# A two-layer hybrid decoder step on one core: all weight chunks rounded on ScalarE, all remainders made on VectorE

## The chip, the cores and the metric

The kernel runs on one core of a Trainium2 chip. The metric is the device time of one execution in microseconds (us). Before the change it was timed three times: 2738.05, 2743.83 and 2746.66 us, median 2743.83 us.

## The reference

The program is one inference step of a two-layer decoder trunk in float32, over a prompt of 1024 tokens and 8 samples of 8 tokens, with model width 1024. Each layer is a mixer and a convolutional feed-forward, both in a sandwich of RMS norms:

```python
for layer in range(2):
    h = rmsnorm(x, norm_pre_mix[layer])
    y = even_mixer(h, ...) if layer == 0 else odd_mixer(h, ...)
    x = x + rmsnorm(y, norm_post_mix[layer])
    h = rmsnorm(x, norm_pre_ffn[layer])
    up = h @ w_up[layer]                                  # 1024 -> 5632
    c = causal_dwconv(up, buf, dw_w, dw_b)                # 3 taps
    g, val = split(c, 2); f = (gelu(g) * val) @ w_down[layer]   # 2816 -> 1024
    x = x + rmsnorm(f, norm_post_ffn[layer])
```

The even mixer is a gated linear attention (4 heads) beside a gated convolution of 31 taps over 512 channels; the odd mixer is a dilated window attention in three groups beside a chunked spatial gating unit. Each has one input projection and one output projection. The outputs are the activations and all new states and caches.

## The kernel before

**Products.** Every large product runs three times at TensorE's faster float32 format: the activation is split into a rounded part `hi` and a remainder `lo`, the weight chunk likewise into `whi` and `wlo`, and `gemm` (L374) adds hi x whi, lo x whi and hi x wlo into one PSUM tile. A weight chunk is up to 8 k-tiles of 128 x 128, a tile of 128 partitions x 1024 float32 (512 or 384 columns where a product has 4 or 3 k-tiles).

**Making a weight chunk.** `chunk` (L355) and `gemm_narrow` call `fill` (L363): SyncE's queue loads the chunk into `raw` (two buffers), one engine rounds `raw` into `whi` (three buffers), one engine subtracts to make `wlo` (three buffers). Which engine does it is told by two knobs in sixteenths that the program sets by stage: `hi_act`, the share of chunks rounded on ScalarE (the rest on GpSimd, L206), and `lo_pool`, the share of remainders made on GpSimd (the rest on VectorE). Both instructions of the remainder carry the line L371; a rounding on ScalarE carries L209.

**Stages.** The prompt is worked in two halves, A (tokens 0 to 511, matmuls of 512 columns) and B (tokens 512 to 1023 and the 64 sample tokens, matmuls of 288 columns). `run` (L1854) puts them in this order: input projection of A, of B, output projection of A, feed-forward of A; output projection of B, input projection of the second layer for A, feed-forward of B, and so on. Beside the products of one half, `during` feeds the other half's pointwise work into the program (convolution, linear attention, attention, norms). The knobs were: from the start to about 62 us all roundings on GpSimd; then to about 840 us all on ScalarE with half of the remainders on GpSimd (16, 8); from there to about 2100 us all roundings on GpSimd and all remainders on VectorE (0, 0), but for 6 of 16 roundings on ScalarE during the second layer's input projection of B; around the second layer's output projection of B, to about 2275 us, all roundings on ScalarE and all remainders on GpSimd (16, 16); after that (0, 0) again.

**Order.** The tile framework orders the instructions of every engine before the run, from a schedule that it simulates, by the order of the program and by priorities: with `ahead = 400` a chunk's load, rounding and remainder stand 400 places ahead. On the chip each engine then works its queue in order, and an instruction that waits holds all behind it.

**Others on these engines.** ScalarE copies products out of PSUM (L209: `u`, `y`, `qkv`), does the activation functions and the `hi` of each split. VectorE does the convolutions (`cv` in the mixer, `c` in the feed-forward, L200), the `lo` of each split (L197) and adds the feed-forward's partial sums. GpSimd adds the squares for the norms (`ss`, L427), copies the convolution's edges (L600 to L618) and scales attention scores (L206, `S`). PSUM has four tiles for products, of which one of A takes one and one of B two.

Of the kernel before, what the change touches and what calls it, by code (L numbers as in the profile page):

```python
# [9 lines left out]
F32 = mybir.dt.float32  # L10
# [3 lines left out]
ALU = mybir.AluOpType  # L14
# [114 lines left out]
class Half:  # L129
    def __init__(self, idx):  # L130
        self.i = idx
        self.t0 = 512 * idx
        self.ns = NS if idx else 0
        self.n = 512 + self.ns
        self.pieces = [(0, 288), (288, 288)] if idx else [(0, 512)]
        self.blocks = [(b * P, P) for b in range(4)] + ([(512, NS)] if idx else [])


class Kern:
    def __init__(self, ctx, tc, I, O):  # L140
        self.tc, self.nc, self.I, self.O = tc, tc.nc, I, O
        self.uid = 0
        pool = lambda name, **kw: ctx.enter_context(tc.tile_pool(name=name, **kw))
        self.cp = pool("cp", bufs=1)
        self.dp = pool("dp", bufs=1, space=DRAM)
        self.ar = [pool("arA", bufs=24), pool("arB", bufs=24)]
        self.wp = pool("wp", bufs=3)
        self.ap = pool("ap", bufs=10)
        self.fp = pool("fp", bufs=2)
        self.np_ = pool("np", bufs=1)  # L150
        self.mp = pool("mp", bufs=2)
        self.pg = pool("pg", bufs=4, space=PSUM)
        self.pm = pool("pm", bufs=4, space=PSUM)
        self.halves = [Half(0), Half(1)]
        self.rr = 0
        self.copy_act = False
        self.urgent = [0, 0]
        self.bg = None
        self.ahead = 0

        self.nw, self.hi_act, self.lo_pool = 0, 0, 0


    def nm(self, s):
# [197 lines left out]

    def fill(self, raw, whi, wlo, w, k0, nk, c0, m):  # L363
        self.wdma(raw[:, :nk, :m], w[k0 * P:(k0 + nk) * P, c0:c0 + m].rearrange("(k p) m -> p k m", p=P))
        self.nw += 1
        if self.nw * self.hi_act % 16 < self.hi_act:
            self.acopy(whi[:, :nk, :m], raw[:, :nk, :m])
        else:
            self.gts(whi[:, :nk, :m], raw[:, :nk, :m], 1.0, 0.0)
        eng = self.nc.gpsimd if self.nw * self.lo_pool % 16 < self.lo_pool else self.nc.vector  # L370
        eng.tensor_tensor(out=wlo[:, :nk, :m], in0=raw[:, :nk, :m], in1=whi[:, :nk, :m].bitcast(F32),  # L371
                          op=ALU.subtract)

    def gemm(self, h, hs, w, k0, c0, m):  # L374

# [1478 lines left out]
    def run(self):  # L1854
        I, O = self.I, self.O
        A, B = self.halves
        self.consts()
        self.S = None
        xs = {(s, h.i): [self.dram([P, h.n], f"x{s}") for _ in range(KT)] for s in range(4) for h in self.halves}

        def norms(h, y, ss, s, post, l, pre, lp, out):

            box = []
            yield from self.post_steps(h, y, ss, xs[s, h.i], post, l, xs[s + 1, h.i], box)
            yield from self.pre_steps(h, y, box[0], pre, lp, out)

        mix_norms = lambda h, y, ss, s, l, out: norms(h, y, ss, s, "norm_post_mix", l, "norm_pre_ffn", l, out)

        QA, QB, QC, QD, QE, QF = 8, 12, 7, 8, 6, 8

        st = ({}, {})
        load = self.load_x(A, xs[0, 0], st[0])
        vec = self.vec_consts()
        next(load)
        next(vec)
        for _ in vec:
            pass
        for _ in load:
            pass
        self.during(self.load_x(B, xs[0, 1], st[1]), 9, LQ)  # L1880
        self.in_even(A, st[0]["hs"], st[0], ("u",))
        self.ahead = 400
        self.drain()
        self.mix_consts()
        self.hi_act, self.lo_pool = 16, 8
        self.during(self.conv(A, st[0]), 90, 30)
        self.in_even(A, st[0]["hs"], st[0], ("glr", "q", "k", "v0", "v1", "r"))
        rest = self.merge((self.bg, 50), (self.gla(A, st[0]), 45))
        self.bg = None
        self.during(rest, 95, VQ)  # L1890
        self.in_even(B, st[1]["hs"], st[1], VB1)
        self.drain()
        y, ss = self.out_proj(A, st[0]["gl"] + st[0]["cv"], I["w_out_even"][0])
        hA = []
        self.urgent[0] = 1
        self.during(mix_norms(A, y, ss, 0, 0, hA), 18, QA)
        self.in_even(B, st[1]["hs"], st[1], VB2)
        self.drain()
        self.urgent = [0, 0]
        self.conv_state(B, st[1])  # L1900

        def mix0():
            yield from self.merge((self.conv(B, st[1]), 120), (self.gla(B, st[1]), 52), (self.cache_rows(), 48),
                                  (self.ffn_state(0), 3))

        self.during(mix0(), 210, 61)
        y, ss = self.ffn(A, hA, 0)
        self.drain()
        self.hi_act, self.lo_pool = 0, 0
        hA = []  # L1910
        self.urgent[0] = 1
        for _ in norms(A, y, ss, 1, "norm_post_ffn", 0, "norm_pre_mix", 1, hA):
            pass
        self.urgent = [0, 0]
        y, ss = self.out_proj(B, st[1]["gl"] + st[1]["cv"], I["w_out_even"][0])
        hB = []


        def prepare():
            yield from self.odd_consts()  # L1920
            yield from self.sgu_prepare()

        self.during(self.merge((prepare(), 6), (mix_norms(B, y, ss, 0, 0, hB), 18)), 24, QB)
        so = {0: self.in_odd(A, hA)}
        self.drain()

        def mix1(h):
            if not h.i:
                yield from self.sample_masks(h)
                yield from self.gmlp(h, so[h.i])  # L1930
            if h.ns:
                yield from self.sample_attention(h, so[1])
            yield from self.attention(h, so[h.i], so[0])
            oc = so[h.i]["oc"]
            if h.ns:
                for hp in range(2):
                    self.nc.vector.tensor_copy(oc[hp][:, 512:], so[1]["ocs"][:, hp, :])
            so[h.i]["mo"] = oc + so[h.i]["du"]

        nxt = {}  # L1940

        def close_a():
            self.drain()
            y, ss = self.out_proj(A, so[0]["mo"], I["w_out_odd"][0])
            nxt["hA"] = []
            self.during(mix_norms(A, y, ss, 2, 1, nxt["hA"]), 18, QC)

        self.during(mix1(A), 63, 50)
        y, ss = self.ffn(B, hB, 0, {3.5: close_a})
        hB = []  # L1950
        self.urgent[1] = 1
        self.during(norms(B, y, ss, 1, "norm_post_ffn", 0, "norm_pre_mix", 1, hB), 18, QD)

        def odd_b():
            self.drain()
            self.urgent = [0, 0]
            act = lambda shape: self.ap.tile(shape, F32, tag="act", name=self.nm("sg"))
            self.copy_act, self.hi_act = True, 6
            so[1] = self.in_odd(B, hB, lambda st: self.during(self.merge((self.gmlp(B, st, act), 11), (self.sample_scores(B, st), 48)), 59, QS))
            self.drain()  # L1960
            self.ffn_rows(0)
            self.copy_act, self.hi_act = False, 0
            self.during(mix1(B), QM, 45)

        def close_b():
            self.drain()
            self.hi_act, self.lo_pool = 16, 16
            y, ss = self.out_proj(B, so[1]["mo"], I["w_out_odd"][0])
            nxt["hB"] = []
            self.urgent[1] = 1  # L1970
            self.during(self.merge((mix_norms(B, y, ss, 2, 1, nxt["hB"]), 18), (self.ffn_state(1), 3.3)), 21.3, QE)

        y, ss = self.ffn(A, nxt["hA"], 1, {0.5: odd_b, 4: close_b})
        self.drain()
        self.urgent = [0, 0]
        self.hi_act, self.lo_pool = 0, 0
        rows = []

        def end_a():
            yield from self.finish(A, y, ss, xs[3, 0])  # L1980
            yield from self.x_rows(B, A, xs[3, 1], rows)

        self.during(end_a(), 19, QF)

        def last(acts, part, y):
            self.ffn_rows(1)
            self.last_down(B, A, acts, 1, part, y, rows)

        self.ffn(B, nxt["hB"], 1, last=last)
# [24 lines left out]
```

## Time and profile before

| | before |
|---|---|
| median of three runs | 2743.83 us |
| the profiled execution's own time | 2735.78 us |
| its span | 2733.9 us |
| TensorE, VectorE, ScalarE, GpSimd busy | 95%, 64%, 35%, 37% |
| mean granted TensorE clock | 0.97 |

The profile is of one execution; its span runs from the first instruction to the last. Engines: PE is TensorE's matmul, DVE VectorE, ACT ScalarE, POOL GpSimd. A group of instructions is told as line, engine, operation, tiles out<-in and shape, then count, busy us, mean ns, and the idle time of the engine just before them with what ended it.

### The profile page before, as it was taken

Reading aid. Unit: us, or ns where it says so; the run is one execution under the profiler, and the core shown is the slowest. Engines: PE = TensorE matmul, PEld = TensorE weight load, DVE = VectorE, ACT = ScalarE, POOL = GpSimd, SP = SyncE. Lnnn points to the kernel's source line nnn. Section 1 sums busy time; section 2 is a strip of 40 time slices with the busy share of each in tenths; the row PEclk is TensorE's granted clock in tenths of the full one; section 3 lists DMA queues with packets and bytes.
Section 4 is the critical chain, followed back from the end, with each engine's and each line's share of the span. In section 5 each row is a group of like instructions: output and inputs, shape, how many; then the busy total and the mean of one; then the engine's idle time right before and its main releaser. Section 6 shows DMA issues by size and latency. Waiting matters only on the chain.

```text
span 2733.9 us, 43963 instructions
## 1 busy us (share of the span) xinstructions
PE 2601.8 (95%) x16517; PEld 2327.2 (85%) x16517; DVE 1753.5 (64%) x3065; ACT 961.9 (35%) x2022; POOL 1023.1 (37%) x1139
## 2 busy tenths in 40 slices
PE   7989999999999999999999999889999898999998
PEld 6779787787888779999999979878878678999998
DVE  4897359999677653655557784547665358555555
ACT  4343445443453222333323242113333343322223
POOL 2311333342235443243437533553113266333333
PEclk9999989999999999999999999999999799999999
DMA  7433354454544454332324336884454152422232
GB/s 218 127 99 92 90 188 151 138 159 159 179 142 126 152 179 117 117 97 81 89 70 137 122 112 191 234 237 133 131 162 137 34 172 84 140 78 75 81 91 82
DMA packets 505004, 355.83 MB, mean 130 GB/s; under 512 B 29547, under 2 KB 461282, under 8 KB 504015
## 3 DMA queue, kind: packets, MB, share of 16 engines
q1 hardware_dynamic: 504791, 353.01, 42.7%
q8 instruction: 131, 2.15, 0.3%
q14 instruction: 82, 0.67, 0.1%
HBM read 306.43 MB, written 75.97 MB: 140 GB/s over the span
## 4 chain that ended last, share of the span: by engine, by line
PE 73%; DVE 10%; DMA 7%; POOL 4%; issue 3%; ACT 2%; SPq 1%; DVEq 0%; POOLq 0%; ACTq 0%
PE g L227 65%; PE m L227 7%; DVE cv L200 3%; PE m L224 2%; DMA kc<-qr 2%; DVE wlo L371 1%; SPq L188 1%; POOL whi L206 1%; DVE y L200 1%; DVE c L200 1%; POOL ss L427 1%; POOL w L1692 1%; DVE lo L197 1%; DVE y L197 1%; POOL wlo L371 1%
## 5 line engine op out<-in xcount | busy, mean ns | idle before, releaser
L227 PE MATMUL g<-hi,whi 128*128 128x288 f32 (+2 forms) x4440 | 1276.7, 336 | 25.7 <-DVE y L197 9.3
L227 PE MATMUL g<-lo,whi 128*128 128x288 f32 (+2 forms) x4440 | 1263.5, 333 | 5.4 <-DVE lo L197 5.3
L227 PE MATMUL g<-hi,wlo 128*128 128x288 f32 (+1 forms) x4416 | 1254.4, 333 | 9.8 <-POOL wlo L371 6.6
L227 PEld LDWEIGHTS g<-hi,whi 128*128 128x128 f32 (+1 forms) x4440 | 776.5, 191 | 100.0 <-issue 25.9
L227 PEld LDWEIGHTS g<-lo,whi 128*128 128x128 f32 (+1 forms) x4440 | 775.3, 191 | 69.2 <-DVE lo L197 7.5
L227 PEld LDWEIGHTS g<-hi,wlo 128*128 128x128 f32 x4416 | 771.5, 191 | 72.5 <-POOL wlo L371 7.0
L371 DVE TENSOR_TENSOR wlo<-raw,whi 128x1024 fp32r<-128x1024 f32 (+2 forms) x382 | 408.1, 1069 | 443.0 <-POOL whi L206 346.1
L206 POOL TENSOR_SCALAR whi<-raw 128x1024 fp32r<-128x1024 f32 (+2 forms) x307 | 313.7, 1022 | 708.8 <-PE g L227 589.2
L371 POOL TENSOR_TENSOR wlo<-raw,whi 128x1024 fp32r<-128x1024 f32 (+2 forms) x94 | 205.0, 2182 | 417.0 <-ACT whi L209 357.1
L200 DVE SCALAR_TENSOR_TENSOR c<-u,dw,c 128x512 f32<-128x512 f32 (+3 forms) x528 | 318.7, 641 | 47.1 <-ACT c L212 45.7
L209 ACT ACTIVATE whi<-raw 128x1024 fp32r<-128x1024 f32 (+3 forms) x171 | 145.1, 849 | 362.8 <-PE g L227 189.4
L209 ACT ACTIVATE u<-g 128x224 f32<-128x224 f32 (+2 forms) x352 | 128.7, 397 | 299.9 <-PE g L227 286.4
L200 DVE SCALAR_TENSOR_TENSOR cv<-u,cvw,cv 128x512 f32<-128x512 f32 (+21 forms) x240 | 193.3, 815 | 1.8
L197 DVE TENSOR_TENSOR y<-y,g 128x288 f32<-128x288 f32 (+3 forms) x240 | 120.3, 526 | 107.2 <-PE g L227 106.9
L212 ACT ACTIVATE c<-g,dw 128x288 f32<-128x288 f32 (+1 forms) x264 | 172.9, 657 | 2.6 <-DVE lo L197 1.5
L427 POOL TENSOR_TENSOR ss<-ss,sq 128x512 f32<-128x512 f32 (+1 forms) x75 | 120.8, 1611 | 42.7 <-ACT sq L212 41.4
L209 ACT ACTIVATE hi<-c 128x512 fp32r<-128x512 f32 (+1 forms) x88 | 57.9, 658 | 209.1 <-DVE c L197 208.7
L212 ACT ACTIVATE c<-c 128x512 f32<-128x512 f32 (+1 forms) x88 | 57.9, 658 | 142.2 <-DVE c L200 138.3
L600 POOL COPY last<-u 128x2 f32<-128x2 f32 x88 | 49.9, 568 | 120.8 <-ACT u L209 118.0
L200 DVE SCALAR_TENSOR_TENSOR y<-y,vec,rb 128x512 f32<-128x512 f32 (+1 forms) x104 | 88.3, 915 | 7.1 <-ACT rb L209 7.1
L212 ACT ACTIVATE sq<-y 128x512 f32<-128x512 f32 (+3 forms) x103 | 63.1, 622 | 82.9 <-POOL ss L427 43.9
L1692 POOL TENSOR_TENSOR w<-kc,kc 128x512 f32<-128x512 f32 x48 | 65.2, 1372 | 70.7 <-DMA kc<-qr 58.6
(288 smaller groups left out, 2208.7 us busy)
## 6 DMA issues: line engine op xcount, KB each, us to landing
raw<-in_w_up SPq DMA_DIRECT2D x176, 512.0 KB
raw<-in_w_down SPq DMA_DIRECT2D x128, 256.0 KB
raw<-in_w_in_odd SPq DMA_DIRECT2D x44, 512.0 KB
raw<-in_w_in_even SPq DMA_DIRECT2D x40, 512.0 KB
out_s_kv<-in_cache_c_w SPq DMA_DIRECT2D x32, 512.0 KB
raw<-in_w_down SPq DMA_DIRECT2D x64, 192.0 KB
xl<-x SPq DMA_DIRECT2D x40, 256.0 KB
kc<-in_cache_c_w SPq DMA_DIRECT2D x80, 128.0 KB
```

Of the source, the lines that this page charges most:

```text
L188: self.nc.sync.dma_start(out, in_)
L197: self.nc.vector.tensor_tensor(out=out, in0=a, in1=b, op=op)
L200: self.nc.vector.scalar_tensor_tensor(out=out, in0=a, scalar=s, in1=b, op0=op0, op1=op1)
L206: self.nc.gpsimd.tensor_scalar(out=out, in0=a, scalar1=s1, scalar2=s2, op0=op0, op1=op1)
L209: self.nc.scalar.activation(out, in_, AF.Copy, scale=scale)
L212: self.nc.scalar.activation(out, in_, func, **kw)
L224: self.nc.tensor.transpose(out, in_, self.ident[:k, :k])
L227: self.nc.tensor.matmul(out, l, r, start=start, stop=stop)
L371: eng.tensor_tensor(out=wlo[:, :nk, :m], in0=raw[:, :nk, :m], in1=whi[:, :nk, :m].bitcast(F32), op=ALU.subtract)
L427: eng.tensor_tensor(out=t, in0=t, in1=sq, op=ALU.add)
L600: self.nc.gpsimd.tensor_copy(self.last2[l][:, jt, :], u[:, 512:514])
L1692: nc.gpsimd.tensor_tensor(out=pr, in0=kc.rearrange("p i c -> p (i c)"), in1=q.rearrange("p i c -> p (i c)"), op=ALU.mult)
```

## The change

`fill` always rounds on ScalarE and always makes the remainder on VectorE; the knobs and the chunk counter go.

```diff
-        self.nw, self.hi_act, self.lo_pool = 0, 0, 0
...
     def fill(self, raw, whi, wlo, w, k0, nk, c0, m):
         self.wdma(raw[:, :nk, :m], w[k0 * P:(k0 + nk) * P, c0:c0 + m].rearrange("(k p) m -> p k m", p=P))
-        self.nw += 1
-        if self.nw * self.hi_act % 16 < self.hi_act:
-            self.acopy(whi[:, :nk, :m], raw[:, :nk, :m])
-        else:
-            self.gts(whi[:, :nk, :m], raw[:, :nk, :m], 1.0, 0.0)
-        eng = self.nc.gpsimd if self.nw * self.lo_pool % 16 < self.lo_pool else self.nc.vector
-        eng.tensor_tensor(out=wlo[:, :nk, :m], in0=raw[:, :nk, :m], in1=whi[:, :nk, :m].bitcast(F32),
-                          op=ALU.subtract)
+        self.acopy(whi[:, :nk, :m], raw[:, :nk, :m])
+        self.tt(wlo[:, :nk, :m], raw[:, :nk, :m], whi[:, :nk, :m].bitcast(F32), ALU.subtract)
...
-        self.hi_act, self.lo_pool = 16, 8
...
-            self.copy_act, self.hi_act = True, 6
+            self.copy_act = True
...
-            self.hi_act, self.lo_pool = 16, 16
```

## Rows read from the trace of the kernel before

**Rows 1.** The page's table of engines: busy us, share of the span, instructions.

```profile
PE 2601.8 (95%) x16517; PEld 2327.2 (85%) x16517; DVE 1753.5 (64%) x3065; ACT 961.9 (35%) x2022; POOL 1023.1 (37%) x1139
```

**Rows 2.** Stages: length, PE, PEld, DVE, ACT, POOL busy (count), clock, DMA, GB/s.

```profile
62.00:840.00 778.00, 738.64 (x4119) 624.76 (x4120) 605.05 (x1070) 329.55 (x608) 236.11 (x162) 0.96 0.44 137
840.00:2100.00 1260.00, 1216.79 (x7797) 1096.59 (x7793) 769.07 (x1322) 397.33 (x869) 515.18 (x601) 0.98 0.47 138
2100.00:2275.00 175.00, 152.53 (x1045) 124.10 (x1045) 87.11 (x174) 72.52 (x152) 72.83 (x71) 0.86 0.35 109
2275.00:2734.00 459.00, 446.46 (x3342) 443.39 (x3340) 263.49 (x447) 135.86 (x332) 182.39 (x286) 0.99 0.31 91
```

**Rows 3.** Waits of PE in those stages in order: total us, times, longest.

```profile
PE g L227 <- POOL wlo L371: 6.6, 1, 6.6
...
PE m L227 <- POOL ss L427: 2.9, 1, 2.9
...
PE m L227 <- POOL ss L427: 3.4, 1, 3.4
...
PE m L227 <- POOL ss L427: 3.5, 1, 3.5
```

**Rows 4.** Timeline of POOL and of DVE, 526 to 548 us: start, us, instruction.

```profile
530.56 13.08 POOL L371 TENSOR_TENSOR wlo<-raw,whi 128x1024 fp32r<-128x1024 f32 x1 [4.26 <-ACT whi L209]
...
526.74 1.21 DVE L371 TENSOR_TENSOR wlo<-raw,whi 128x1024 fp32r<-128x1024 f32 x1
527.88 0.28 DVE L983 COPY_PREDICATED AT<-lev,m 64x64 f32<-64x64 int8 x1
...
539.71 0.27 DVE L200 SCALAR_TENSOR_TENSOR cv<-us,cvw,cv 128x64 f32<-128x64 f32 x1
...
540.04 0.73 DVE L200 SCALAR_TENSOR_TENSOR cv<-u,cvw,cv 128x512 f32<-128x512 f32 x1
...
541.36 2.35 DVE L200 SCALAR_TENSOR_TENSOR cv<-us,cvw,cv 128x64 f32<-128x64 f32 x1
```

**Rows 5.** Timeline of POOL near 370, 880 and 2240 us.

```profile
365.93 7.33 POOL L371 TENSOR_TENSOR wlo<-raw,whi 128x1024 fp32r<-128x1024 f32 x1 [11.14 <-ACT whi L209]
...
874.87 6.94 POOL L206 TENSOR_SCALAR whi<-raw 128x1024 fp32r<-128x1024 f32 x1 [3.13 <-PE g L227]
...
2237.80 1.45 POOL L371 TENSOR_TENSOR wlo<-raw,whi 128x384 fp32r<-128x384 f32 x1
```

**Rows 6.** L371 and L206 by operation: count, ns min/median/max, first and last start.

```profile
L371 POOL TENSOR_TENSOR wlo<-raw,whi x94: 995/1852/13077, 68.9 to 2272.3; 128x1024 fp32r<-128x1024 f32 x46, 128x512 fp32r<-128x512 f32 x24, 128x384 fp32r<-128x384 f32 x24
...
L206 POOL TENSOR_SCALAR whi<-raw x307: 506/1045/6942, 14.5 to 2691.1; 128x1024 fp32r<-128x1024 f32 x90, 128x512 fp32r<-128x512 f32 x52, 128x384 fp32r<-128x384 f32 x12
```

**Rows 7.** Groups by shape, 62 to 840 us.

```profile
L371 POOL TENSOR_TENSOR wlo<-raw,whi 128x1024 fp32r<-128x1024 f32 x42 | 135.1, 3217 | 256.7 <-ACT whi L209 247.2 <-PE m L227 8.6 <-PE g L227 0.9
L371 POOL TENSOR_TENSOR wlo<-raw,whi 128x512 fp32r<-128x512 f32 x16 | 22.9, 1432 | 63.7 <-ACT whi L209 40.2 <-PE g L227 17.1 <-DVE cv L200 6.4
L371 POOL TENSOR_TENSOR wlo<-raw,whi 128x384 fp32r<-128x384 f32 x8 | 8.3, 1043 | 17.7 <-ACT whi L209 17.7
...
L209 ACT ACTIVATE whi<-raw 128x1024 fp32r<-128x1024 f32 x84 | 88.9, 1059 | 193.4 <-PE g L227 85.0 <-DMA raw<-in_w_up 51.4 <-DMA raw<-in_w_in_even 21.9
...
L200 DVE SCALAR_TENSOR_TENSOR cv<-u,cvw,cv 128x512 f32<-128x512 f32 x120 | 96.5, 804 | 0.1
L200 DVE SCALAR_TENSOR_TENSOR cv<-us,cvw,cv 128x64 f32<-128x64 f32 x120 | 57.5, 479 | 0.0
```

**Rows 8.** Timeline of ACT in the first 65 us.

```profile
25.16 1.69 ACT L209 ACTIVATE hi<-x 128x512 fp32r<-128x512 f32 x3
```

**Rows 9.** Groups by shape, 840 to 2100 us.

```profile
L206 POOL TENSOR_SCALAR whi<-raw 128x1024 fp32r<-128x1024 f32 x127 | 165.6, 1304 | 311.5 <-PE g L227 253.8 <-DMA raw<-in_w_in_odd 24.6 <-DMA raw<-in_w_up 13.6
```

More of the change, by code (lines that the diff above doesn't have):

```diff
@@ L1908, in run @@
         self.drain()
-        self.hi_act, self.lo_pool = 0, 0
         hA = []
@@ L1961, in odd_b @@
             self.ffn_rows(0)
-            self.copy_act, self.hi_act = False, 0
+            self.copy_act = False
             self.during(mix1(B), QM, 45)
@@ L1975, in run @@
         self.urgent = [0, 0]
-        self.hi_act, self.lo_pool = 0, 0
         rows = []
```

## The prediction

> **What bounds the kernel now.** I read the table of engines first, then the stages in windows, then the waits of TensorE, then the timelines of GpSimd and VectorE where TensorE waited, and last the groups of instructions that the change moves. TensorE is busy for 95% of the span, VectorE for 64%, ScalarE for 35%, GpSimd for 37% [rows 1]: no total of another engine sets the time, so the change can only act through the places where TensorE stands still, and through the order of the queues.
>
> The stages differ [rows 2]. From 62 to 840 us TensorE is busy 738.6 of 778 us, and VectorE, which carries the two causal convolutions and the linear attention beside the weights, 605 us (78%). From 840 to 2100 us it is 1216.8 of 1260 for TensorE and 61% for VectorE, ScalarE only 32%. From 2100 to 2275 us TensorE is down to 152.5 of 175 at a granted clock of 0.86. After 2275 us TensorE is busy 446.5 of 459 us and nothing can be won. So all that this change can win or lose lies in some 40 + 43 + 22 us of TensorE's idle time before 2275 us.
>
> Two things are to be seen in the waits. Several of the longest of TensorE end on GpSimd: 6.6 us on a remainder that GpSimd made, and 2.9, 3.4 and 3.5 us on the sums of squares that GpSimd adds [rows 3]. And in three of the four GpSimd was late because one of its weight instructions ran far over its usual time while VectorE worked without a pause: the remainder at 530.56 us took 13.08 us [rows 4], the one at 365.93 us 7.33 us, a rounding at 874.87 us 6.94 us [rows 5], against medians of 1.85 us for a remainder and 1.05 us for a rounding [rows 6]. The two engines hold each other up: while that 13.08 us remainder ran, VectorE's instructions kept their usual 0.73 and 0.27 us until the last of them, of the 0.27 us kind, took 2.35 us [rows 4].
>
> **The change part by part.**
>
> *Remainders from GpSimd to VectorE, 62 to 840 us.* GpSimd makes 42 of 1024 columns, 16 of 512 and 8 of 384 there [rows 7]. On VectorE one of 1024 takes 1.21 us and the next instruction starts 1.14 us after it [rows 4]; by columns I estimate 0.6 and 0.5 us for the smaller. That adds 42 x 1.14 + 16 x 0.6 + 8 x 0.5 = 62 us to VectorE. What it loses again is its own waiting for GpSimd. The 64-column convolution steps have a mean of 0.479 us over 120, against 0.27 undisturbed: 120 x 0.21 = 25 us; the 512-column steps 0.804 against 0.73: 9 us [rows 4, 7]. Those two groups are 154 of VectorE's 605 us and already give 34 us; the rest of its work in the stage, which met the same GpSimd instructions, I put at 25 to 35 us more, an estimate from the held-up instruction of rows 4 (2.1 us lost for one large remainder): 42 x 2.1 = 88 us is the ceiling of the large ones. So VectorE's load in this stage changes by 62 - 60 = about 0; the bounds are +28 (only the 34 us come back) and -26 (the whole 88).
>
> What remains on the path is the lateness. The wait of 6.6 us at 543.7 us goes; next late there is VectorE itself, whose convolution steps follow each other without a pause, so I count 4 of the 6.6 us (bounds 0 and 6.6). The wait of 2.9 us on the sum of squares near 379 us stood behind the 7.33 us remainder; the sums themselves are two-input additions on GpSimd, and wait for VectorE likewise, so I count 2 (0 to 2.9).
>
> *Remainders, 2100 to 2275 us.* Here all go from GpSimd to VectorE, 94 in all less the 66 above, 28 [rows 6, 7], most of them of 512 and 384 columns: some 16 us for VectorE, which is busy 87 of 175 us [rows 2]. The sum of squares that TensorE waits 3.5 us for stands right behind a remainder of 1.45 us that started at 2237.80 us [rows 3, 5]: I count 2 us won (0 to 3.5), and 1 us lost where the normalisation is a chain on VectorE and a remainder steps in between (0 to 4).
>
> *Roundings from GpSimd to ScalarE, in the first 62 us, from 840 to 2100 and after 2275 us.* There are 307 [rows 6]; ScalarE takes 1.06 us for 1024 columns [rows 7], so it gains at most 325 us and goes from 35% to at most 47%. That lies beside TensorE's work: in the stage from 62 to 840 us ScalarE already rounds every chunk, at 329.6 of 778 us busy, and none of TensorE's listed waits there names a rounding. The price is delay, not load. ScalarE also copies the products out of PSUM, and a rounding ahead of a copy holds it for 1.06 us; the four PSUM buffers give TensorE about one product of 48 matmuls to spare, 48 x 0.137 = 6.6 us by the last stage of rows 2, so this is hidden. It isn't hidden where ScalarE's own chain is what TensorE waits for: at the start, where the splits of x follow each other from 25.16 us without a pause [rows 8], and in the six normalisations between sub-layers. One rounding of 1.06 us in each of these seven is 7 us (bounds 0 and 15, two in each). I count 5, since some of them have a product of the other half beside them.
>
> What comes back: the 6.94 us rounding in front of the sums of squares before 890 us leaves GpSimd's queue; of the 3.4 us that TensorE waited for them I count 2 [rows 3, 5]. VectorE is held up less: the 127 roundings of 1024 columns from 840 to 2100 us have a mean of 1.30 us against the median of 1.05 [rows 6, 9], so 127 x 0.25 = 32 us of mutual waiting, of which I put a tenth on the path, 3 us (0 to 10). The latency of a chunk becomes steadier too, since no remainder waits any more for a rounding of up to 6.94 us: 3 us more, an allowance for TensorE's waits too small to be listed (0 to 8).
>
> *Sum.* Won: 4 + 2 + 2 + 2 + 3 + 3 = 16. Lost: 5 + 1 = 6. Net 10 us, of the profiled execution's 2735.8 us (span 2733.9). That execution lies 8 us under the median of the runs shown, 2743.8; the same 10 us off that median gives **2734 us**. What I can't price by rows is the order itself: the framework lays out every queue anew from a simulated schedule in which the engines' loads have changed, and TensorE's queue is in order. From the idle 105 us before 2275 us I allow 15 us either way for it.
>
> **The rule weighed.** In the trace the 13.08 us remainder and VectorE's instructions ran at the same time, VectorE's at their usual length, until one was held for 2.1 us [rows 4]. The Trainium skill, page SBUF — State Buffer, section "SBUF: two separate sides", says that VectorE's second read port and GpSimd share a pair of ports as an exclusive lock, held by whoever starts first for the whole instruction, the other blocking fully. By that rule a remainder would cost VectorE all of its own time; by the row it costs what is left when it at last gets through. The rule's sum for the first stage would be the rival called lock below.
>
> **The rivals.**
> *No gain on the path (same).* TensorE's place is taken by the next late one everywhere: VectorE at 543 us, the sums of squares, still on GpSimd beside a VectorE with 28 + 66 more remainders. For it speaks that VectorE's load in the saturated stage doesn't fall by my own sum; against it, that the waits of rows 3 end on GpSimd by name. Then 16 becomes 7, less 6: 2743 us.
> *ScalarE blocked by transfers (slower).* A rounding waits for its chunk to land, and with it wait all copies out of PSUM behind it in ScalarE's queue. In the first stage ScalarE stood 51.4 and 21.9 us for chunks of two weights [rows 7]; from 840 to 2100 us it is GpSimd that stands 24.6 and 13.6 us so [rows 9], where it held nobody up. It decides from the point where one such wait exceeds the 6.6 us of a product. If two thirds of these 38 us come through to TensorE, 25 us, with the 10 won kept, 15 us are lost: 2759 us. It would show between 1650 and 1850 us, where the caches load. Against it: in the first stage ScalarE's 73 us of such waits appear in none of TensorE's.
> *The lock (much faster).* If GpSimd's remainders cost VectorE their whole time in the first stage, 135.1 + 22.9 + 8.3 = 166 us come back for 62 added: 104 us less for an engine that I take as the bound in a third of that stage, so 35 us on the path: 2709 us. Rows 4 speak against it.
>
> **How the numbers follow.** What a measurement of this kernel can tell from no change is about 0.3%, 8 us. The forecast 0.35, no gain 0.33, ScalarE blocked 0.25, the lock 0.07. The forecast sits near the bound, so of its 0.35 I put 0.31 to faster and 0.04 to same; of "no gain" 0.03 to faster and 0.01 to slower. Faster: 0.31 + 0.03 + 0.07 = 0.41. Same 0.04 + 0.29 = 0.33. Slower 0.26. The forecast's own range is 2718 to 2750; the range, which reaches to both outer rivals with the 15 us of the order, 2706 to 2768.
>
> **What would show it.** Right: no remainder or rounding on GpSimd; VectorE's 64-column convolution steps back from a mean of 0.479 to near 0.27 us, and its busy time from 62 to 840 us within 30 us of 605; no wait of TensorE on a GpSimd remainder, and shorter ones on the sums of squares; ScalarE near 46% busy. Wrong: new waits of TensorE on ScalarE's copies with ScalarE standing for a chunk's transfer (the second rival), or longer waits on VectorE's remainders from 440 to 700 us, which would say that the convolutions and the remainders now stand in each other's way.

## The result

The changed kernel takes 2678.73 us (median of 4 runs, 2674.56 to 2683.46), the kernel before 2745.24 us beside it (2738.05 to 2748.60): a ratio of 0.9766, 95% interval 0.9744 to 0.9789. It is 66.5 us faster, where 10 were forecast, and outside the predicted range. The profiled execution took 2676.47 us, 59.3 less than that of before; its span is 2674.7 us.

The page of the changed kernel: engines, and the shares of the chain that ended last (of before, the chain had PE 73%, DVE 10%, POOL 4%).

```profile
PE 2595.2 (97%) x16517; PEld 2317.8 (87%) x16517; DVE 1703.4 (64%) x3160; ACT 1211.8 (45%) x2341; POOL 487.0 (18%) x729
...
PE 84%; DMA 6%; DVE 3%; ACT 2%; issue 2%; POOL 1%; SPq 1%; DVEq 0%; POOLq 0%; ACTq 0%
```

VectorE carries 95 more instructions and is busy 50 us less [rows 1]. To see where the time came from, both kernels were cut where TensorE had begun the same number of matmuls of the large products (those into the tiles `g`, 13440 in all): 500, 1000, 1750, 2750 and 3240. The stage from 62 us to the 3240th of them in windows, kernel before (columns as in [rows 2]):

```profile
62.00:148.10 86.10, 82.99 (x374) 66.60 (x374) 72.32 (x90) 29.57 (x43) 28.16 (x10) 1.00 0.42 122
148.10:251.10 103.00, 92.25 (x746) 87.02 (x745) 95.77 (x179) 39.82 (x78) 15.45 (x10) 0.93 0.31 91
251.10:422.60 171.50, 159.81 (x949) 143.19 (x948) 82.10 (x163) 81.69 (x162) 52.59 (x35) 0.92 0.46 148
422.60:697.80 275.20, 261.39 (x1299) 211.01 (x1298) 262.32 (x468) 112.71 (x185) 95.34 (x57) 0.96 0.45 144
697.80:838.00 140.20, 140.20 (x732) 115.33 (x731) 92.24 (x174) 65.46 (x140) 42.58 (x49) 0.98 0.47 150
```

The same products in the changed kernel:

```profile
62.00:148.40 86.40, 86.40 (x390) 69.62 (x389) 70.52 (x100) 30.31 (x44) 7.98 (x6) 1.00 0.48 138
148.40:237.90 89.50, 83.71 (x728) 80.12 (x727) 84.01 (x174) 39.02 (x77) 1.42 (x1) 1.00 0.33 97
237.90:404.90 167.00, 159.13 (x966) 140.85 (x965) 94.21 (x183) 80.50 (x161) 26.95 (x24) 0.94 0.48 150
404.90:665.60 260.70, 259.66 (x1335) 209.92 (x1334) 252.43 (x508) 117.91 (x200) 33.97 (x38) 1.00 0.51 159
665.60:804.90 139.30, 139.30 (x737) 114.78 (x736) 93.52 (x182) 64.19 (x131) 17.16 (x27) 0.98 0.47 145
```

Read the length, which stands behind the bounds, together with VectorE's busy time, the third of the busy times. Two slices gave 28 of the 33 us: the second (103.0 to 89.5) and the fourth (275.2 to 260.7). They are those in which VectorE was busy 93% and 95% of the time; there it got lighter by 11.8 and 9.9 us, though it makes all the remainders. In the third slice, where it was busy 48%, it got heavier by 12.1 us and the slice still became shorter. I call the two *full slices* and the third the *idle slice*.

Beyond this stage there were two more places, in both kernels the normalisations between sub-layers (before, then after):

```profile
838.00:1011.40 173.40, 161.70 (x902) 139.08 (x901) 117.81 (x151) 51.66 (x93) 90.25 (x54) 0.96 0.50 156
2009.80:2273.60 263.80, 241.11 (x1620) 194.08 (x1619) 141.88 (x295) 103.66 (x221) 97.06 (x111) 0.90 0.38 116
```

```profile
804.90:963.50 158.60, 155.33 (x863) 135.24 (x862) 103.33 (x148) 73.20 (x116) 49.41 (x27) 0.98 0.54 168
1965.90:2217.10 251.20, 243.51 (x1590) 193.06 (x1589) 135.81 (x303) 113.47 (x228) 53.52 (x67) 0.93 0.38 115
```

That is 14.8 and 12.6 us. The last product comes 59.5 us earlier (2723.9 to 2664.4 us), and these two with the 33.1 us of the stage are the whole of it; in the rest of the program some 6 us come and go. In a second profiled execution of the changed kernel the stage takes 740.3 us and these two stretches 160.5 and 245.7, so differences of 2 to 6 us in one place say nothing by themselves.

VectorE's groups in the stage, changed kernel (62 to 804 us; they correspond to [rows 7]):

```profile
L195 DVE TENSOR_TENSOR wlo<-raw,whi 128x1024 fp32r<-128x1024 f32 x85 | 104.7, 1232 | 66.3 <-ACT whi L207 65.6
L198 DVE SCALAR_TENSOR_TENSOR cv<-u,cvw,cv 128x512 f32<-128x512 f32 x120 | 89.1, 744 | 0.3 <-ACT cv L210 0.3
L198 DVE SCALAR_TENSOR_TENSOR cv<-us,cvw,cv 128x64 f32<-128x64 f32 x120 | 32.7, 277 | 0.0
```

The 64-column steps fell from 479 to 277 ns, the 512-column steps from 804 to 744. TensorE's waits in the stage (total us, times, longest):

```profile
PE m L222 <- DVE w L201: 3.7, 1, 3.7
PE g L225 <- ACT th L210: 3.5, 2, 3.0
PE m L225 <- DVE tot L195: 2.3, 1, 2.3
PE m L222 <- ACT us L207: 1.5, 1, 1.5
PE g L225 <- ACT hi L207: 1.3, 1, 1.3
PE m L225 <- POOL ss L419: 1.3, 1, 1.3
```

Of the kernel before, beside those of [rows 3], there were:

```profile
PE g L227 <- ACT hi L209: 4.7, 3, 3.0
PE m L227 <- DVE tot L197: 3.9, 1, 3.9
...
PE m L227 <- DMA glr<-zglr: 3.6, 1, 3.6
```

The two waits that end on GpSimd by name fell from 9.5 to 1.3 us, by 8 us. TensorE's idle time in the stage fell from 39.4 us (776.0 less 736.6) to 14.7: the larger part was under other names.

### The profile page after: what moved, and what is told of

The parts are those of the page before. It is cut to its first block, busy times and chain, and to the rows that moved or that the text cites. A ratio compares the mean times of both kernels' runs of the same rounds, so it can differ in the third digit from the quotient of the medians.

```text
span 2674.7 us, 43807 instructions
## 1 busy us (share of the span) xinstructions
PE 2595.2 (97%) x16517; PEld 2317.8 (87%) x16517; DVE 1703.4 (64%) x3160; ACT 1211.8 (45%) x2341; POOL 487.0 (18%) x729
## 4 chain that ended last, share of the span: by engine, by line
PE 84%; DMA 6%; DVE 3%; ACT 2%; issue 2%; POOL 1%; SPq 1%; DVEq 0%; POOLq 0%; ACTq 0%
PE g L225 75%; PE m L225 7%; PE m L222 2%; DMA kc<-qr 1%; DMA kc<-in_cache_c_w 1%; SPq L186 1%; POOL ss L419 1%; DVE lo L195 0%; DVE wlo L195 0%; ACT sq L210 0%; DVE y L198 0%; DMA raw<-in_w_down 0%; DMA out_p_kv<-rows 0%; ACT whi L207 0%; DMA v<-zv 0%
## 5 line engine op out<-in xcount | busy, mean ns | idle before, releaser
L225 PE MATMUL g<-hi,whi 128*128 128x288 f32 (+2 forms) x4440 | 1271.1, 334 | 16.6 <-ACT c L210 6.4
L207 ACT ACTIVATE whi<-raw 128x1024 fp32r<-128x1024 f32 (+3 forms) x478 | 412.9, 865 | 874.5 <-PE g L225 698.5
L195 DVE TENSOR_TENSOR wlo<-raw,whi 128x1024 fp32r<-128x1024 f32 (+2 forms) x476 | 479.8, 1009 | 451.4 <-ACT whi L207 442.6
L198 DVE SCALAR_TENSOR_TENSOR c<-u,dw,c 128x512 f32<-128x512 f32 (+3 forms) x528 | 298.5, 602 | 55.5 <-ACT c L210 53.7
L592 POOL COPY last<-u 128x2 f32<-128x2 f32 x88 | 70.0, 796 | 657.5 <-ACT u L207 652.0
L419 POOL TENSOR_TENSOR ss<-ss,sq 128x512 f32<-128x512 f32 (+1 forms) x75 | 132.6, 1769 | 267.5 <-ACT sq L210 266.9
L198 DVE SCALAR_TENSOR_TENSOR cv<-u,cvw,cv 128x512 f32<-128x512 f32 (+16 forms) x240 | 173.8, 740 | 1.5 <-ACT cv L210 0.3
L609 POOL COPY lastp<-u 128x2 f32<-128x2 f32 x88 | 39.1, 444 | 451.2 <-ACT u L207 451.2
L195 DVE TENSOR_TENSOR lo<-c,hi 128x512 fp32r<-128x512 f32 (+1 forms) x88 | 64.1, 728 | 28.5 <-ACT hi L207 28.1
L198 DVE SCALAR_TENSOR_TENSOR y<-y,vec,rb 128x512 f32<-128x512 f32 (+1 forms) x104 | 78.0, 817 | 3.9 <-ACT rb L207 3.9
```

The source lines that it names most:

```text
L195: self.nc.vector.tensor_tensor(out=out, in0=a, in1=b, op=op)
L198: self.nc.vector.scalar_tensor_tensor(out=out, in0=a, scalar=s, in1=b, op0=op0, op1=op1)
L207: self.nc.scalar.activation(out, in_, AF.Copy, scale=scale)
L225: self.nc.tensor.matmul(out, l, r, start=start, stop=stop)
L419: eng.tensor_tensor(out=t, in0=t, in1=sq, op=ALU.add)
L592: self.nc.gpsimd.tensor_copy(self.last2[l][:, jt, :], u[:, 512:514])
```

## The experiments

The theory: while GpSimd runs a weight instruction, VectorE's instructions take longer; where VectorE has no time to spare, that and the late chunk go straight into TensorE's time. The rivals: that the new order of the queues did it, or that a remainder on GpSimd is simply late wherever it is made.

**The two halves of the change.** First the remainders alone, in the kernel before:

```diff
-        eng = self.nc.gpsimd if self.nw * self.lo_pool % 16 < self.lo_pool else self.nc.vector
+        eng = self.nc.vector
```

> The remainders' part alone: every remainder on VectorE, the roundings shared between ScalarE and GpSimd as before. Theory 1 (GpSimd's remainders were late beside a VectorE that worked without a pause, and the products of the stage from 62 to 840 us stood behind them): the 36 us of that stage and most of the 9 us between 2100 and 2290 us come back here, the 12 us at 840 to 1011 us do not; about 2700 us, 45 us under before (2690 to 2710). Theory 2 (the gain comes from the new order that the framework laid out for every queue, whichever part is changed): no such pattern by place; anywhere from 2680 to 2745 us, and the gain at the product that before reaches at 763 us differs from 36 us by more than 15.

Measured: 2686.98 us (2685.74 to 2687.31), ratio 0.9812 (0.9792 to 0.9833), better than the first theory had it. The stage takes 738.3 us (776.0 before), and of the stretch from 2010 us 12.7 us go. The gain of the stage stands in the same slices as with the whole change. About the order this says little: in the first full slice TensorE's queue stands in the same order as in the changed kernel, and in the second it differs in 192 places. One thing came that was not expected: the stretch from 838 us, in which no instruction was edited, is 8.0 us shorter too (165.4 us, 173.4 before; it begins at 800.3 us in this run), at the same busy time of VectorE:

```profile
800.30:965.70 165.40, 157.17 (x862) 136.08 (x861) 117.78 (x146) 51.02 (x91) 82.31 (x51) 0.97 0.51 159
```

Then the roundings alone:

```diff
-        if self.nw * self.hi_act % 16 < self.hi_act:
+        if True:
```

> The roundings' part alone: every rounding on ScalarE, the remainders shared between VectorE and GpSimd as before. Theory 1: nothing is won from 62 to 840 us, where the roundings were on ScalarE already; about 12 us from 840 to 1011 us, where a rounding of 6.94 us stood ahead of the sums of squares; 2730 us (2720 to 2740). Theory 2: the order is new here too, so the stage from 62 to 840 us changes by more than 10 us either way.

Measured: 2729.95 us, ratio 0.9962 (0.9945 to 0.9980). The stage is unchanged (775.9 us); 12.1 us come at 838 us:

```profile
837.90:999.20 161.30, 157.17 (x902) 137.00 (x901) 99.99 (x154) 74.50 (x117) 58.87 (x28) 0.98 0.54 167
```

VectorE is busy 17.8 us less there than before, and TensorE's waits that name VectorE fell there from 8.2 to 0.3 us; the one on GpSimd's sums of squares stayed (3.4 and 3.9 us). At the last product the halves nearly add up: 49.5 and 12.3 us, 59.5 for both together. By place they do not: in the stretch from 838 us 8.0 and 12.1 stand against 14.8, so how much of the 12.1 us is the roundings' and how much the new order's is not separated.

**GpSimd's work without its result.** Into the changed kernel, from 62 to about 805 us, an extra GpSimd instruction for every second chunk (66) was put; it writes a scratch tile that nothing reads:

```diff
+        if self.extra and m == P and self.nw % 2:
+            x, y = raw[:, :nk, :m], whi[:, :nk, :m].bitcast(F32)
+            self.nc.gpsimd.tensor_tensor(out=self.junk[:, :nk, :m], in0=y, in1=y, op=ALU.subtract)
```

> The changed kernel with one more instruction on GpSimd for every second chunk from 62 to about 805 us: it subtracts the rounded chunk from itself into a scratch tile that nobody reads, the size of the remainder that GpSimd made before. Nothing waits for its result, but it reads two tiles at the same time as VectorE works. Theory 1a (GpSimd beside VectorE lengthens VectorE's instructions, and that was the 36 us of this stage): 20 to 36 us come back as loss, 2700 to 2715 us, the 64-column convolution steps back from 277 ns towards 479. Theory 1b (the products waited for the late remainder itself, not for a slower VectorE): the steps lengthen the same, but the time stays within 10 us of the changed kernel, 2679 to 2690 us. Theory 2 (order): also within 10 us.

Measured: 2718.26 us (2714.66 to 2720.72), 40 us slower than the changed kernel and a little above the 2700 to 2715 of theory 1a, though nothing waits for what was added. Its groups in the stage, and its windows over the idle slice and the second full slice:

```profile
L370 POOL TENSOR_TENSOR junk<-whi 128x1024 bf16<-128x1024 f32 x42 | 128.4, 3058 | 241.7 <-ACT whi L208 241.7
...
L199 DVE SCALAR_TENSOR_TENSOR cv<-us,cvw,cv 128x64 f32<-128x64 f32 x120 | 50.8, 427 | 0.0
```

```profile
248.20:423.20 175.00, 163.27 (x967) 144.75 (x965) 98.81 (x186) 80.72 (x161) 56.11 (x35) 0.91 0.46 143
423.20:706.60 283.40, 268.13 (x1335) 212.37 (x1334) 280.17 (x499) 118.07 (x197) 120.45 (x61) 0.98 0.45 146
```

The 64-column steps are back at 427 ns, and in the second full slice VectorE has 27.7 us more and the slice 22.7; in the first it is 10.9 and 9.8. VectorE's idle time in the two slices did not grow (5.5 to 4.4 and 8.3 to 3.2 us), so what GpSimd's own later work may have lost does not explain them. Nor does the order: by the traces TensorE's 16517 matmuls stand in the order of the changed kernel but for 96 places, none of them in the first full slice and 6 in the second. The other 90 are in the idle slice, which became 8.0 us longer, though VectorE is busy 56% there. TensorE's waits on GpSimd's sums of squares grew there from 1.3 to 3.2 us, those on VectorE's `us` from none to 1.5, and the granted clock fell from 0.94 to 0.91; GpSimd, VectorE and the order are not separated in that slice. Waits of TensorE that the change had ended are back too:

```profile
PE g L226 <- ACT hi L208: 6.2, 3, 3.4
PE m L226 <- DMA glr<-zglr: 4.1, 1, 4.1
```

Then the same, but reading the load buffer (`in0=x`):

> As the run before, but the extra instruction reads the loaded chunk and the rounded one, as the remainder on GpSimd did, and so also keeps the load buffer, of which there are two, until it is through. Theory 1b in the form that the chunk's buffers were freed late: 15 to 36 us slower than the changed kernel, and at least 10 us slower than the run that reads only the rounded chunk. Theory 1a: as that run within 5 us. Theory 2: both within 10 us of the changed kernel.

Measured: 2750.51 us, 72 us slower than the changed kernel and slower than before (ratio 1.0040, 1.0024 to 1.0056). As theory 1b has it, this is over 10 us slower than the run above; the loss is beyond its 36 us. TensorE now also waits for late roundings (1.4 us in the run above); the load buffer is held until the extra instruction is through:

```profile
PE g L226 <- ACT whi L208: 9.4, 4, 5.3
```

VectorE is busy 20 us more in the stage than in the run above. Of the 32 us between the two runs 20 are in the stage, where TensorE's order is almost the same up to the last slice; which of the two, the held buffer or two different tiles to read, makes them was not separated. Another 11 come after 2010 us, where nothing was edited and the order differs.

**Is it the order, and is it GpSimd?** The same extra instruction as a copy on ScalarE:

```diff
+            self.acopy(self.junk[:, :nk, :m], whi[:, :nk, :m].bitcast(F32))
```

> A control for the order: the changed kernel with the same 66 extra instructions for every second chunk from 62 to about 805 us, but as copies of the rounded chunk on ScalarE, which is busy 331 of 742 us there. Theory 1a (GpSimd beside a saturated VectorE lengthens VectorE's instructions): VectorE's steps stay at 277 and 744 ns, the time stays within 8 us of the changed kernel, 2677 to 2687 us. Theory 2 (the 40 us that the extra subtraction on GpSimd cost came from the order that the framework laid out around an extra instruction): 2700 us or more.

Measured: 2684.75 us (2679.20 to 2689.21); in the stage 58 us of copies on ScalarE, and VectorE's steps as they were:

```profile
L208 ACT ACTIVATE junk<-whi 128x1024 bf16<-128x1024 f32 x42 | 44.2, 1052 | 0.4
...
L199 DVE SCALAR_TENSOR_TENSOR cv<-us,cvw,cv 128x64 f32<-128x64 f32 x120 | 33.0, 275 | 0.0
```

So the stage (741.4 us) lost nothing by an extra instruction and a new order. The whole is 6 us slower than the changed kernel, but its interval (0.9775 to 0.9848) meets that kernel's. Most of what the profile shows comes after 1966 us, where nothing was edited. In that stretch, 251.2 and 245.7 us in the changed kernel, two runs keep the changed kernel's order of TensorE's matmuls: the extra subtraction of `whi` above and the one in the feed-forward of B below; they take 249.9 and 249.4 us. Five have another order there, though nothing was edited in it: the one on the load buffer, the two copies and the two with remainders by slice; they take 254 to 261. So the order has a part in this stretch, of 3 to 15 us. As a copy with one input on GpSimd:

```diff
+            self.nc.gpsimd.tensor_copy(self.junk[:, :nk, :m], whi[:, :nk, :m].bitcast(F32))
```

> As the run with the extra subtraction of the rounded chunk on GpSimd, but the extra instruction is a copy with one input, as the roundings were. If any access of GpSimd's holds VectorE up in proportion to its time (a copy of 1024 columns about 1.05 us, the subtraction 2.4 us at best): 44% of the 40 us, about 2696 us. If it is instructions with two inputs that do (a rounding of before lengthened VectorE by 0.18 us, a remainder by 1.50): 66 times some 0.2 us, 13 us on VectorE at most and under 10 us of time, 2679 to 2689 us.

Measured: 2688.70 us (2687.13 to 2690.55), at the upper end of the second expectation, while VectorE's loss is above the 13 us that it allowed. Of the 10 us beside the changed kernel only 2 are in the stage (745.1 us). The copies of 1024 columns take 1.93 us in the mean (1.04 the fastest), and VectorE loses 21 us in the stage (615.6 against 594.7), where the subtraction with two inputs cost it 61:

```profile
L369 POOL CAST junk<-whi 128x1024 bf16<-128x1024 f32 x42 | 81.1, 1930 | 242.1 <-ACT whi L208 242.1
...
L199 DVE SCALAR_TENSOR_TENSOR cv<-us,cvw,cv 128x64 f32<-128x64 f32 x120 | 37.8, 322 | 0.1
```

**The same dose elsewhere.** The extra subtraction, moved to the feed-forward of B (`self.extra` is set around it, 50 instructions):

> The changed kernel with the extra subtraction on GpSimd for every second chunk not in the first stage but in the first layer's feed-forward of B and the second layer's output projection of A inside it (about 1011 to 1530 us), where VectorE is busy some 59% and TensorE 98%. Theory 1a with the condition that VectorE must have no time to spare: VectorE is lengthened by 20 to 40 us all the same, but the time rises by under 6 us, 2677 to 2685 us. If GpSimd beside VectorE costs time wherever it is: 20 us or more, 2700 us.

Measured: 2680.21 us (2672.38 to 2683.98), no loss clear of the noise. From 1011 to 1530 us, the changed kernel and then this one:

```profile
1011.00:1530.00 519.00, 512.84 (x3724) 489.05 (x3723) 307.29 (x639) 250.09 (x532) 119.11 (x241) 1.00 0.34 103
```

```profile
1011.00:1530.00 519.00, 509.97 (x3704) 486.01 (x3703) 338.18 (x639) 248.74 (x531) 206.59 (x289) 1.00 0.34 101
```

VectorE lost 31 us, and the last products came 1.5 us later: at 59% VectorE could afford it.

**Real remainders, by slice.** In the changed kernel 32 remainders went back to GpSimd, all of them where VectorE has time to spare:

```diff
+        eng = self.nc.gpsimd if 36 <= self.nw < 54 or 111 <= self.nw < 125 else self.nc.vector
```

> The changed kernel with 32 remainders of the first stage made on GpSimd again, all of them where VectorE has time to spare in the changed kernel (products made from about 250 to 376 us and from 668 to 728 us; VectorE busy 20 to 80% there). Theory 1 (what counts is VectorE's load in the stretches where it is full, not over the stage): within 6 us of the changed kernel, 2676 to 2685 us, although half as many remainders are back on GpSimd as before the change had there (66). Rival (a remainder on GpSimd is late by itself, 2.4 us for 1.2 and the load buffer held, wherever it is made): half of the 42 us of the stage, 2698 us.

Then 31, every second one where it is full:

```diff
+        eng = self.nc.gpsimd if (28 <= self.nw < 35 or 55 <= self.nw < 109) and self.nw % 2 == 0 else self.nc.vector
```

> The complement: 31 remainders of the first stage on GpSimd, every second one where VectorE is full (about 190 to 235 us and 410 to 660 us). Theory 1: VectorE is relieved of some 30 us of remainders there and loses as much or more by waiting, and the chunks come late: most of the loss of the stage comes back, 20 to 40 us, 2698 to 2718 us. Rival: as the run before, 2698 us in both.

The changed kernel was measured once more with these two (2677.37 us, 2674.19 to 2687.42, where 2679 was expected):

> The changed kernel as it is, beside the others of this call on one chip: 2679 us, 2674 to 2684.

Measured: the idle slices 2686.52 us (2677.51 to 2691.36), just above the 2676 to 2685 expected, the full slices 2706.85 us (2702.22 to 2713.62), as expected. Windows over the idle slice and the second full slice, first with the remainders in the idle slices:

```profile
239.30:409.20 169.90, 160.05 (x966) 142.59 (x965) 76.94 (x166) 81.80 (x163) 69.21 (x42) 0.93 0.47 148
409.20:666.20 257.00, 257.00 (x1334) 209.03 (x1333) 248.09 (x499) 116.75 (x197) 38.57 (x33) 1.00 0.50 159
```

and in the full ones:

```profile
240.20:406.70 166.50, 157.47 (x958) 140.09 (x957) 92.68 (x182) 80.47 (x161) 26.89 (x24) 0.94 0.48 148
406.70:683.50 276.80, 259.87 (x1300) 209.28 (x1299) 261.10 (x466) 116.15 (x190) 92.28 (x59) 0.98 0.46 146
```

In the idle slice 18 remainders took 17 us off VectorE and cost 2.9 us; over the whole stage it is 743.6 us against 742.9 for all 32, and the rest comes after 1966 us as in the run with ScalarE's copies. In the second full slice 27 remainders on GpSimd, as many as the kernel before made there, *added* 8.7 us to VectorE, which makes fewer of them, and 16.1 us to the slice; the other 7.4 us are VectorE's own idle time (8.3 to 15.7 us), which I read as the lateness. The whole stage takes 761.4 us, 18.5 more for 31 remainders; some 4 more us come from 805 to 963 us and some 7 after 1966 us, with another order. The orders of these two runs differ from each other in the full slices too, so the size of the difference is less sure than its sign. The long one is there again, 13.08 us as in [rows 4], in the timeline of GpSimd, with TensorE's wait for a remainder below it:

```profile
514.72 13.08 POOL L367 TENSOR_TENSOR wlo<-raw,whi 128x1024 fp32r<-128x1024 f32 x1 [4.27 <-ACT whi L208]
```

```profile
PE g L226 <- POOL wlo L367: 6.2, 1, 6.2
```

All runs by slice, length and VectorE's busy time in us:

| run | first full slice | idle slice | second full slice |
|---|---|---|---|
| before | 103.0, 95.8 | 171.5, 82.1 | 275.2, 262.3 |
| changed | 89.5, 84.0 | 167.0, 94.2 | 260.7, 252.4 |
| remainders alone | 89.5, 84.0 | 166.9, 94.2 | 257.8, 248.8 |
| roundings alone | 101.4, 94.7 | 169.0, 82.5 | 275.2, 262.5 |
| extra subtraction, GpSimd | 99.3, 94.9 | 175.0, 98.8 | 283.4, 280.2 |
| the same, load buffer | 104.0, 100.3 | 176.8, 98.9 | 296.6, 289.5 |
| extra copy, ScalarE | 90.5, 84.0 | 168.1, 93.8 | 258.0, 246.7 |
| extra copy, GpSimd | 91.2, 87.1 | 168.5, 97.9 | 263.3, 257.3 |
| GpSimd in idle slices | 90.7, 84.1 | 169.9, 76.9 | 257.0, 248.1 |
| GpSimd in full slices | 92.0, 86.5 | 166.5, 92.7 | 276.8, 261.1 |

In the full slices the length follows VectorE's busy time, with 3 to 16 us beside it; in the idle slice VectorE's time varies by 22 us, and the slice is shortest at 92.7 and at 94.2, not at 76.9. It is longest in the two runs with the extra subtraction, as told above.

**A version that beats both.** Among the two-input work that stays on GpSimd are the sums of squares:

```diff
-        eng = self.nc.vector if k % len(ss) else self.nc.gpsimd
-        eng.tensor_tensor(out=t, in0=t, in1=sq, op=ALU.add)
+        self.tt(t, t, sq, ALU.add)
```

> The changed kernel with the sums of squares for the norms added on VectorE too (75 two-input additions; GpSimd keeps the copies of edges and the scores). They lengthen VectorE's instructions by some 25 us in the changed kernel, and TensorE still waits 7.9 us for them. Theory 1: VectorE takes some 57 us more and gets 25 back, mostly where it has time to spare; TensorE's waits on the sums go or move to VectorE; 2670 us (2660 to 2682), the best of all if right. Rival: in the normalisations VectorE's own chain is what TensorE waits for, and the additions stand in it: 2685 us or more.

Measured: 2666.28 us (2664.06 to 2667.71), ratio 0.9744 (0.9717 to 0.9772). Since that interval meets the changed kernel's, the two were measured again side by side:

> The changed kernel with the sums of squares added on VectorE, a second time beside the changed kernel: 2667 us, 9 to 15 us under the changed kernel of this call, if the 12 us seen between calls are the edit's and not the chip's.

2665.39 us (2657.58 to 2666.62), ratio 0.9716 (0.9699 to 0.9734) against 0.9772 (0.9752 to 0.9793) for the changed kernel: 12 us faster both times. All 87 additions are VectorE's (groups of the second run):

```profile
L195 DVE TENSOR_TENSOR ss<-ss,sq 128x512 f32<-128x512 f32 x47 | 31.8, 686 | 2.7 <-ACT sq L210 2.6
...
L195 DVE TENSOR_TENSOR ss<-ss,sq 128x576 f32<-128x576 f32 x40 | 29.9, 751 | 6.9 <-ACT sq L210 6.8
```

They take 0.69 to 0.75 us each, where GpSimd took 1.60 to 1.97 in the changed kernel, and VectorE's busy total rises by only 14 us (1703.4 to 1717.2). By the last profile some 5 to 8 us are won in the stage and 10 to 15 from 1522 to 1966 us, and the two normalisations after 805 and after 1966 us became longer by 4 to 10 us each; the order changed in all of them, so the cause of the 12 us is not shown.

## Why the prediction was wrong

The direction was right, and most of the mechanism; the gain was more than six times the forecast. What was named as its signs came: the 64-column steps at 277 ns, VectorE within 30 us of 605, no wait on a GpSimd remainder, ScalarE at 45%; the waits on the sums shrank least, from 9.8 to 7.9 us in three. Step by step:

**The failed step: "VectorE's load in this stage changes by 62 - 60 = about 0"**, with no term in the sum. As an average it held: 604.8 to 594.7 us, -10, within the bounds of +28 and -26. The remainders added 62.8 us (134.7 less 71.9) and VectorE got 73 back, where 60 were put. But the two sides fell into different slices, and the sum priced their average; only the sum of the lock rival took VectorE as the bound in a part of the stage. What came back came where VectorE was full, -21.7 us in the two full slices; in the idle slice it rose by 12.1 us, and cost nothing there. The full slices became 28 us shorter, and the sum had 0 for them. The extra subtraction shows it in the order of the changed kernel (9.8 and 22.7 us in the full slices), and the remainders by slice agree: 32 in the idle slices cost 0.7 us of the stage, 31 in the full ones 18.5. Windows a third as long over the kernel before show 95% where [rows 2] shows 78%. The Trainium skill, page Perfetto Trace Analysis, section "Optimization Strategy", says that the most-contended engine can change over time and that its gaps are to be looked for within the regime in question; the slices above agree: VectorE is busy 93% and 95% beside TensorE's 90% and 95% in the full ones, and 48% beside 93% in the idle one.

**Lateness, 4 + 2 us.** The wait of 6.6 us went, and so did most of that on the sums near 379 us. The step counted only waits that end on GpSimd by name, 8 us of 25 in the stage. The others named ScalarE, VectorE and a DMA, and two of them, on ScalarE's `hi` and on the transfer of `glr`, came back in the run with the extra subtraction, for whose result nobody waits.

**TensorE's clock, not in the sum.** In the first full slice TensorE was busy 92.25 us, and 83.71 in the changed kernel; 18 fewer small matmuls fall into it there. The same 500 matmuls of the large products took 75.8 us at a mean granted clock of 0.93 before, and 70.3 at 1.00 after (these matmuls alone, with the few that reach over the bounds):

```profile
148.10:251.10 103.00, 75.78 (x502) 70.40 (x501) 0.00 (x0) 7.66 (x21) 0.93 0.31 91
...
148.40:237.90 89.50, 70.30 (x502) 65.88 (x501) 0.00 (x0) 7.68 (x21) 1.00 0.33 97
```

Windows over the kernel before:

```profile
140.00:150.00 10.00, 10.00 (x54) 8.68 (x53) 9.64 (x12) 1.70 (x3) 0.76 (x1) 1.00 0.53 159
150.00:160.00 10.00, 6.42 (x28) 4.43 (x27) 9.75 (x11) 4.79 (x8) 2.50 (x1) 0.84 0.75 238
160.00:170.00 10.00, 10.00 (x70) 9.84 (x71) 6.01 (x9) 8.71 (x10) 0.00 (x0) 0.82 0.48 163
170.00:180.00 10.00, 8.22 (x76) 8.03 (x74) 8.85 (x13) 6.32 (x13) 3.54 (x4) 1.00 0.20 55
```

It stood 3.6 us in the second of these, and was granted 0.84 and 0.82 there and in the next, partly 1.2 instead of 2.4 GHz. Over the stage its busy time fell by 8.4 us, with 56 matmuls more in it and a mean granted clock of 0.98 instead of 0.96, on top of the 24.7 us of idle time: a third as much again.

**2100 to 2275 us, 2 - 1 us.** The stretch gave 12.6 us, and as much with the remainders alone. TensorE's idle time there fell from 22.7 to 7.7 us, but with the remainders alone only to 17.8, with a busy time 7.8 us shorter. The order of TensorE's queue is new in both, and has a part of 3 to 15 us in this stretch; so the term, read from one wait of 3.5 us, was too small, but what made the 12.6 us stays open.

**Roundings.** Won 2 + 3 + 3, lost 5, net 3; measured 12.3 at the last product. The mutual waiting was put at 32 us from 840 to 2100 us, a tenth on the path; in the normalisation at 838 us alone VectorE got 17.8 us back, and 12.1 came through, less what the order made of it. The 2 us on the sums were not among them: that wait stayed. ScalarE in seven chain places: the first product began 0.8 us later, of the others nothing is to be seen.

**The order, 15 us either way.** It was there: 8.0 us from 838 us with the remainders alone, and 3 to 15 us from 1966 us in kernels edited only before 805 us. In the full slices the loss came back without it, with the extra subtraction.

**The range.** It is said to reach both outer rivals with the 15 us of the order. From 2709 and 2759 us that gives 2694 to 2774, not 2706 to 2768; neither holds the 2678.73 us.

**The rivals.** "No gain" was wrong: VectorE was not the next late one, it was the late one. ScalarE blocked by transfers: from 1522 to 1966 us ScalarE stood 16.6 and 12.2 us for chunks of two weights, and none of TensorE's listed waits there names a weight's rounding. The lock came nearest in time, by luck: VectorE lost 73 us to GpSimd's 166 us of remainders, not 166; it was right in one thing, that VectorE bounds part of the stage. The rule behind it, in the Trainium skill, page SBUF — State Buffer, section "Who interferes with whom", has a VectorE instruction with two SBUF inputs contend with GpSimd's reads, and ScalarE wait for nobody: the runs agree in that (VectorE lost 61 us and 21 us to GpSimd and nothing to ScalarE, whose copies of 1024 columns took 1.05 us). It has the loser blocked for the whole of the other's instruction: of the recorded time VectorE lost a third, 61 us for 178 us of subtractions. But that time seems to hold GpSimd's own waiting as well: the subtractions of 1024 columns took 1.89 us at the fastest and 3.06 in the mean. In [rows 4] VectorE was held 2.1 us at the end of a remainder of 13.08 us, whose kind takes 2.34 us at the fastest. So the runs do not show that the rule fails, only that the recorded time is not its price.

## What to carry to other kernels

Add up loads by stretches short enough that the engine is either full or not, and price an edit first where it is full: 28 us more on VectorE cost 23 us in the second full slice, 31 us cost 1.5 in the feed-forward of B. A half-idle engine is not always free, though: the idle slice became 8.0 us longer with the extra subtraction, for a cause that was not separated. Where an engine is full, its lateness appears in TensorE's waits under the names of whoever depends on it, so a count by name is a lower bound, and the stalls cost a second time in TensorE's granted clock. GpSimd is no free helper for two-input work beside a full VectorE; beside one at 59%, in the feed-forward of B, it nearly was.

## What the runs showed of the hardware

- A two-input GpSimd instruction on 384 to 1024 columns cost VectorE 0.92 us in the first stage (61 us for 66) and 0.64 in the feed-forward of B (31 for 48), a one-input copy 0.32 us (21 for 66), the same copy on ScalarE nothing (591.3 against 594.7 us busy).
- It goes both ways: on GpSimd the copy of 1024 columns took 1.04 us at the fastest and 1.93 in the mean of the first stage, and the subtraction 3.06 us in that mean against 2.62 us in the feed-forward of B. Real remainders of 1024 columns took 2.42 us in the idle slices and 3.48 in the full ones.
- The longest remainder recurs: 13.08 us at 530.56 us in the kernel before and 13.08 us at 514.72 us in the run with the remainders in the full slices.
